# Expert layers of a two-block transformer: how many down units are kept during routing, and which engine builds the gated one-hot rows

## The chip, the cores and the metric

The kernel runs on one core of a Trainium2 chip. The metric is the device time of one execution in microseconds. Three executions of the kernel before gave 3460.87, 3461.62 and 3469.74 us; the median is 3461.62 us. Engines are named as the profile names them: PE (matmul) with PEld (its weight loads), DVE (vector), ACT (scalar), POOL (GpSimd), SP (which issues the DMAs).

## The reference, cut to what matters

Two layers of a first block, each a mixer and an expert layer, are followed by two layers of a second block (feed-forward, mixer, feed-forward). The change is in the expert layers alone. An expert layer scores 256 tokens against two sets of 128 sub-keys in 8 heads, takes the best 16 pairs in each head, and for those experts (16384 = 128 x 128 in all) computes a gated sum:

```python
def chunk(xi):
    q = (xi @ w_query).reshape(B, PEER_CHUNK, PEER_HEADS, 2, PEER_HALF)
    s = jnp.einsum('bthpd,hpnd->bthpn', q, sub_keys)
    s1, i1 = lax.top_k(s[..., 0, :], PEER_TOPK)
    s2, i2 = lax.top_k(s[..., 1, :], PEER_TOPK)
    cand = (s1[..., :, None] + s2[..., None, :]).reshape(...)
    top_s, top_c = lax.top_k(cand, PEER_TOPK)
    idx = (jnp.take_along_axis(i1, top_c // PEER_TOPK, axis=-1) * PEER_N_KEYS
           + jnp.take_along_axis(i2, top_c % PEER_TOPK, axis=-1))
    g = jax.nn.softmax(top_s.astype(jnp.float32), axis=-1)
    u = jnp.take(expert_down, idx, axis=0)
    act = jax.nn.gelu(jnp.einsum('btd,bthkd->bthk', xi, u).astype(jnp.float32))
    v_sel = jnp.take(expert_up, idx, axis=0)
    return jnp.einsum('bthk,bthkd->btd', (g * act).astype(xi.dtype), v_sel)
```

## The kernel before, in words

Nothing is gathered. The kernel computes the down projection of all 16384 experts for all 256 tokens, multiplies it by a gate that is zero for the experts that a token did not choose, and projects all of it up. Expert number 128*i1 + i2 belongs to unit i2; a unit is a block of 128 experts, one 512 KB load of weights (`raw`), split by ACT into a high part `whi` (L93) and by DVE into a low part `wlo` (L97), and 24 matmuls (three products, L170 to L172, for each of 8 chunks of the model width).

One expert layer (`peer`, L488) runs in these stages:

- **Routing.** 16 query units and their scores, then a long chain of small DVE instructions (maxima, indices, gates), which ends in the tile `it` (L610): for each token its 128 selected pairs as two key numbers and a gate. PE has little to do in that chain, so the first `N_STORE` = 64 units of the down projection are computed meanwhile (`down_pair`, two units to a PSUM bank). ACT takes each pair through the gelu into `ca` (L614), which stays in SBUF.
- **One-hot loop** (L622). The gates are expanded in 64 groups of four tokens. For each token a row block `oa` (selected pair against key number, 1 where the first key number is that column, L631, DVE) and a row block `ob` (the gate where the second key number is that column) are built, 128 x 128 each, by comparing `iota` with a column of `it`. `ob` takes one DVE instruction a token (L636, two per-partition operands) or two ACT instructions (L633, L634): by `by_act` (L628) ACT has the groups whose number leaves 1 when divided by `N_ACT` = 3, which is 21 of 64, DVE the other 43. PE multiplies the two (L639) into a PSUM bank `gps`: the gates of four tokens for all experts. DVE multiplies the part of the first `N_STORE` units into `ca` (L641), and ACT copies the rest into `gg` (L642). `oa` and `ob` have `OH` = 3 buffers each, `gps` rotates over four banks. L641 can't begin before all of `ca` is there.
- **Units after the loop.** For the units from `N_STORE` on, `down_pair` leads to the gelu in place (L665) and a DVE product into `gg` (L667). The first two pairs (`N_PARK`) use the banks that the up projection will accumulate in, and can run beside the loop. Then 32 (first expert layer) or 40 (second) steps of `Mod.step` are due (L670): each loads 512 KB of `w_mod` through the same three `raw` buffers and gives PE 4 matmuls (L940); they compute modulation vectors of the second block and are what PE has to fill the one-hot loop with. After that pairs of down units alternate with up units (`up`, L652), which lag `N_LAG` = 16 units behind.

The order of the instructions on each engine is fixed when the kernel is built, by a planner that goes by priorities and its own estimate of times; on the chip each engine goes through its list in order and waits by semaphores.

Of the kernel before, what the change touches and what calls it, by code (L numbers as in the profile page):

```python
# [19 lines left out]
NDC = 8  # L20
EPS = 1e-6
NEG = -1.0e30
N_STORE = 64
N_LAG = 16
N_PARK = 2
N_MOD = 32
# [2 lines left out]
PAT_1 = "gggv"  # L29
PAT_0 = "gv"  # L30
M_BUFS = 3
N_ACT = 3
OH = 3
AB = 3
AHEAD = 0
# [452 lines left out]
def peer(n: Net, layer, mod, mod_upto):  # L488
    nc, d = n.nc, n.d
    pre = f"l{layer}_"  # L490
    NS = N_STORE
    n.stream.pattern = PAT_R
    with ExitStack() as st:
# [6 lines left out]
        def down_pair(i, sink, tag=None):  # L500
            b = n.bank("dn", tag).rearrange("p (u t) -> p u t", u=2)
            for u in range(2):
                w = n.unit(d[pre + "down"][i + u])
                n.proj_t(b[:, u], w, xn, first=u == 0)
            sink(b)

        with ExitStack() as sr:
# [44 lines left out]
            for a0, a1, wb, o in CAND:  # L552
                na = a1 - a0
                nc.vector.tensor_tensor(
                    out=cand[:, :, o:o + na * wb].rearrange("p h (a b) -> p h a b", b=wb),
                    in0=v4[:, :, 0, a0:a1].unsqueeze(3).to_broadcast([128, 16, na, wb]),
# [56 lines left out]
            for i in range(0, NS, 2):  # L613
                down_pair(i, lambda b: nc.scalar.activation(  # L614
                    out=ca[:, i:i + 2], in_=b, func=AF.Gelu_apprx_tanh), "ac")

        with ExitStack() as sg:
            gp = sg.enter_context(n.tc.tile_pool(name="gg", bufs=1, reuse_waits="tile"))
            gg = gp.tile([128, 128 - NS, T], F32, name="gg")
            onehot = n.tc.tile_pool(name="oneh", bufs=OH, reuse_waits="tile")  # L620
            o2 = onehot.__enter__()
            for t0 in range(0, T, 4):  # L622
                a = o2.tile([128, 4, 128], F32, tag="oa", name="oa")
                b = o2.tile([128, 4, 128], F32, tag="ob", name="ob")
                g = n.bank("gps").rearrange("p (t e) -> p t e", t=4)


                by_act = t0 // 4 % N_ACT == 1  # L628
                for t in range(4):
                    at = lambda s: it[:, s, t0 + t:t0 + t + 1]  # L630
                    nc.vector.tensor_scalar(out=a[:, t], in0=n.iota, scalar1=at(0), scalar2=None, op0=OP.is_equal)  # L631
                    if by_act:
                        nc.scalar.activation(out=b[:, t], in_=n.iota, func=AF.Abs, scale=-1.0, bias=at(1))  # L633
                        nc.scalar.activation(out=b[:, t], in_=b[:, t], func=AF.Relu, scale=-2.0, bias=at(2))  # L634
                    else:
                        nc.vector.tensor_scalar(out=b[:, t], in0=n.iota, scalar1=at(1), scalar2=at(2),  # L636
                                                op0=OP.is_equal, op1=OP.mult)
                for t in range(4):
                    nc.tensor.matmul(g[:, t], a[:, t], b[:, t], start=t == 0, stop=True, skip_group_check=True)  # L639
                ge = g.rearrange("p t e -> p e t")  # L640
                nc.vector.tensor_tensor(out=ca[:, :, t0:t0 + 4], in0=ca[:, :, t0:t0 + 4], in1=ge[:, 0:NS], op=OP.mult)  # L641
                nc.scalar.copy(out=gg[:, :, t0:t0 + 4], in_=ge[:, NS:128])  # L642
            n.stream.pattern = PAT_G
            onehot.__exit__(None, None, None)
            g2 = sg.enter_context(n.tc.tile_pool(name="gg2", bufs=2, reuse_waits="tile"))

            def coef(i):
                return ca[:, i] if i < NS else gg[:, i - NS]

            acc = []  # L650

            def up(i):  # L652
                if not acc:
                    acc.extend(n.accs())
                w = n.unit(d[pre + "up"][i])
                c = coef(i)
                ch = g2.tile([128, T], F32R, tag="ch", name="ch")
                cl = g2.tile([128, T], F32R, tag="cl", name="cl")
                n.split(c, ch, cl)
                n.up(acc, w, (ch, cl), i == 0, i == 127)  # L660

            done = 0
            for i in range(NS, 128, 2):
                def sink(b):
                    nc.scalar.activation(out=b, in_=b, func=AF.Gelu_apprx_tanh)  # L665
                    c = gg[:, i - NS:i - NS + 2]
                    nc.vector.tensor_tensor(out=c, in0=c, in1=b, op=OP.mult)  # L667
                if i == NS + 2 * N_PARK:
                    while mod.next < mod_upto:
                        mod.step(n.main.raw_p)  # L670
                    mod.bank = None
                down_pair(i, sink, "ac" if i < NS + 2 * N_PARK else None)
                while i >= NS + 2 * N_PARK and done < i + 2 - N_LAG:
                    up(done)
                    done += 1
            while done < 128:
                up(done)
                done += 1
            n.residual(n.x, acc)
# [765 lines left out]
def two_blocks_kernel(ctx: ExitStack, tc: tile.TileContext, d, out, stages=None):  # L1445
# [12 lines left out]
    for s in stages:  # L1458
        with tc.tile_pool(name="xn", bufs=1, reuse_waits="tile") as n.xn_p:
            if s in ("mix0", "mix1"):  # L1460
                with n.psum(ac=4, mm=3, fl=1), tc.tile_pool(name="mod", bufs=M_BUFS, reuse_waits="tile") as p:
                    with n.low():
                        aside(mods[0], p, M_0 if s == "mix0" else M_1)
                    (hgrn_gmlp if s == "mix0" else mla_moba)(n)
            elif s.startswith("peer"):
                with n.psum(ac=4, mm=2, m2=2):
                    peer(n, int(s[4]), mods[1], N_MOD if s[4] == "0" else 72)
            elif s.startswith("mod"):
                with n.psum(ac=4, mm=2, fl=2), tc.tile_pool(name="mod", bufs=3, reuse_waits="tile") as p:
                    aside(mods[int(s[3])], p, 72)  # L1470
            elif s.startswith("ffn"):
                w, l = int(s[3]), int(s[5])
                with n.psum(ac=4, mm=2, m2=2):
                    ffn(n, n.x, mods[l], 0, 0 if w == 1 else 6, d[f"f{w}i{l}"], d[f"f{w}o{l}"],
                        n.v(f"norm_g{l}")[:, (w - 1) * 16:(w - 1) * 16 + 8], s)
            elif s == "mixb0":
                with n.psum(ac=4, mm=2, fl=2):
                    window_gla(n, mods[0])
            elif s == "mixb1":
                with n.psum(ac=4, mm=2, m2=2):  # L1480
                    pool_mix(n, mods[1])
            elif s == "final":
                with n.psum(ac=4, mm=2, m2=2):
                    final_norm(n, out)
# [154 lines left out]
```

## Time and profile before

| | us |
|---|---|
| median of three executions | 3461.62 |
| the profiled execution, its own time | 3467.64 |
| its span (first to last instruction) | 3465.9 |
| PE busy / DVE busy / ACT busy / POOL busy | 3313.4 / 2193.9 / 1649.2 / 179.0 |
| one-hot stretch of the first expert layer, after its stored units | 441 to 565 |
| one-hot stretch of the second expert layer, after its stored units | 1529 to 1661 |

The profile is one execution. Times within it are microseconds from the start of the span, unless they are marked ns. Busy time of PE counts the time from a matmul's start to its end, with many matmuls under way at once, so a busy PE need not be at its full rate; the spacing of starts shows the rate. The chain of waits puts 83% of the span on PE and 11% on DVE. Some records of small instructions are missing in a trace (of 64 `ca` products of the first one-hot stretch 61 are listed).

### The profile page before, as it was taken

How to read it: one execution, taken by the hardware profiler on the slowest of the kernel's cores; microseconds unless marked ns; L12 is line 12 of the kernel's file. 1: busy time of each engine (PE TensorE's matmuls, PEld its weight loads, DVE VectorE, ACT ScalarE, POOL GpSimd, SP SyncE). 2: the span in 40 equal slices, each digit the busy share in tenths (PEclk: the TensorE clock that was granted, in tenths of full speed). 3: DMA queues.
4: the chain of work that ended last, by engine and by line, in shares of the span. 5: the costliest groups of instructions: out<-in, count | busy, mean ns of one | idle time of the engine just before them, and what ended most of it. 6: DMA issues, size and time to landing. Idle time of an engine off the chain costs nothing.

```text
span 3465.9 us, 65621 instructions
## 1 busy us (share of the span) xinstructions
PE 3313.4 (96%) x26734; PEld 3150.2 (91%) x26734; DVE 2193.9 (63%) x4589; ACT 1649.2 (48%) x2609; POOL 179.0 (5%) x93
## 2 busy tenths in 40 slices
PE   7999998999999999998999999999999989999798
PEld 6789977999999779996899999999999779999698
DVE  6389487555556559759555555666766656666665
ACT  5445455444444344445445444544644444454443
POOL 2200000000000310000000000100000020100200
PEclk9999999999999999999999999999999999999899
DMA  6645544556555545545556555554444235454353
GB/s 227 230 159 182 178 156 161 183 183 207 183 183 170 199 157 166 177 158 182 195 183 231 183 183 183 182 183 143 158 165 147 86 123 187 165 183 156 132 187 105
DMA packets 165759, 597.79 MB, mean 172 GB/s; under 512 B 18512, under 2 KB 20176, under 8 KB 165072
## 3 DMA queue, kind: packets, MB, share of 16 engines
q1 hardware_dynamic: 165456, 593.59, 51.5%
q8 instruction: 210, 3.44, 0.4%
q14 instruction: 93, 0.76, 0.1%
HBM read 592.47 MB, written 1.05 MB: 171 GB/s over the span
## 4 chain that ended last, share of the span: by engine, by line
PE 83%; DVE 11%; DMA 2%; ACT 2%; issue 1%; POOL 0%; SPq 0%; ACTq 0%; DVEq 0%; POOLq 0%
PE acc L170 11%; PE acc L171 10%; PE acc L172 10%; PE dn L172 7%; PE dn L170 7%; PE dn L171 7%; PE ff L170 6%; PE ff L171 6%; PE ff L172 6%; DVE wlo L97 2%; PE mm L170 2%; PE mm L171 2%; PE mm L172 2%; PE mod L940 2%; DMA mraw<-w_mod 2%; PE gps L639 2%
## 5 line engine op out<-in xcount | busy, mean ns | idle before, releaser
L93 ACT CAST whi<-raw 128x1024 fp32r<-128x1024 f32 x973 | 1016.3, 1046 | 1398.9 <-PE acc L171 540.7
L97 DVE TENSOR_TENSOR wlo<-raw,whi 128x1024 fp32r<-128x1024 f32 x908 | 1111.6, 1225 | 841.8 <-ACT whi L93 841.3
L170 PE MATMUL dn<-xnh,whi 128*128 128x256 f32 x2048 | 582.3, 284 | 3.1 <-ACT gg L642 2.5
L172 PE MATMUL dn<-xnh,wlo 128*128 128x256 f32 x2048 | 581.8, 285 | 1.5 <-DVE wlo L97 1.5
L171 PE MATMUL dn<-xnl,whi 128*128 128x256 f32 x2048 | 581.5, 284 | 0.0
L171 PE MATMUL acc<-cl,whi 128*128 128x256 f32 x2048 | 561.6, 283 | 1.0 <-DVE cl L165 1.0
L172 PE MATMUL acc<-ch,wlo 128*128 128x256 f32 x2048 | 559.5, 283 | 0.0
L170 PE MATMUL acc<-ch,whi 128*128 128x256 f32 x2048 | 512.2, 283 | 0.2 <-DVE gg L667 0.2
L170 PE MATMUL ff<-xnh,whi 128*128 128x258 f32 x1760 | 504.6, 287 | 7.5 <-ACT rstd L216 4.0
L171 PE MATMUL ff<-xnl,whi 128*128 128x258 f32 x1760 | 502.8, 286 | 4.2 <-DVE xnl L247 4.2
L172 PE MATMUL ff<-xnh,wlo 128*128 128x258 f32 x1760 | 499.2, 284 | 3.5 <-POOL wlo L97 2.2
L170 PEld LDWEIGHTS dn<-xnh,whi 128*128 128x128 f32 x2048 | 395.0, 193 | 3.7 <-ACT gg L642 2.7
L172 PEld LDWEIGHTS dn<-xnh,wlo 128*128 128x128 f32 x2048 | 394.4, 193 | 2.2 <-DVE wlo L97 2.2
L171 PEld LDWEIGHTS dn<-xnl,whi 128*128 128x128 f32 x2048 | 395.0, 193 | 0.0
L171 PEld LDWEIGHTS acc<-cl,whi 128*128 128x128 f32 x2048 | 393.2, 192 | 1.5 <-DVE cl L165 1.5
L172 PEld LDWEIGHTS acc<-ch,wlo 128*128 128x128 f32 x2048 | 392.1, 192 | 0.0
L170 PEld LDWEIGHTS acc<-ch,whi 128*128 128x128 f32 x2048 | 363.7, 192 | 0.4 <-DVE gg L667 0.4
L170 PEld LDWEIGHTS ff<-xnh,whi 128*128 128x128 f32 x1760 | 334.8, 190 | 12.2 <-ACT rstd L216 5.2
L171 PEld LDWEIGHTS ff<-xnl,whi 128*128 128x128 f32 x1760 | 337.0, 192 | 6.3 <-DVE xnl L247 5.6
L172 PEld LDWEIGHTS ff<-xnh,wlo 128*128 128x128 f32 x1760 | 335.1, 191 | 4.9 <-POOL wlo L97 2.7
L97 POOL TENSOR_TENSOR wlo<-raw,whi 128x1024 fp32r<-128x1024 f32 (+1 forms) x65 | 157.7, 2433 | 2614.0 <-ACT whi L93 1968.6
L171 PE MATMUL acc<-hl,whi 128*128 128x256 f32 x880 | 246.9, 282 | 3.0 <-DVE hl L1017 3.0
(446 smaller groups left out, 5389.5 us busy)
## 6 DMA issues: line engine op xcount, KB each, us to landing
raw<-l_down SPq DMA_DIRECT2D x256, 512.0 KB, 3.4
raw<-l_up SPq DMA_DIRECT2D x256, 512.0 KB, 3.3
mraw<-w_mod SPq DMA_DIRECT2D x144, 512.0 KB, 4.4
raw<-f1i SPq DMA_DIRECT2D x132, 512.0 KB, 3.4
raw<-f2i SPq DMA_DIRECT2D x88, 512.0 KB, 3.9
raw<-f1o SPq DMA_DIRECT2D x66, 512.0 KB, 3.3
raw<-w_t SPq DMA_DIRECT2D x46, 512.0 KB, 3.6
raw<-f2o SPq DMA_DIRECT2D x44, 512.0 KB, 4.1
```

The source lines that it names most:

```text
L93: nc.scalar.copy(hi[:, 0:k], raw[:, 0:k])
L97: eng.tensor_tensor(out=low[:, 0:k], in0=raw[:, 0:k], in1=hi.bitcast(F32)[:, 0:k], op=OP.subtract)
L170: mm(out, w[0], x[0], start=first, stop=False, skip_group_check=True)
L171: mm(out, w[0], x[1], start=False, stop=False, skip_group_check=True)
L172: mm(out, w[1], x[0], start=False, stop=last, skip_group_check=True)
L639: nc.tensor.matmul(g[:, t], a[:, t], b[:, t], start=t == 0, stop=True, skip_group_check=True)
L940: nc.tensor.matmul(ps[32 * j:32 * j + 32], n.cond[:, k], raw[:, j * T:(j + 1) * T], start=k == 0, stop=k == NDC - 1, tile_position=(0, 32 ...
```

## The change

Three edits. `N_STORE` goes from 64 to 40: 24 units of each expert layer move from the stage before the one-hot loop to the stage after it, `ca` becomes 40 units wide and `gg` 88. `N_ACT` goes from 3 to 4: ACT builds `ob` for 16 groups of 64 instead of 21. The other 48 groups' `ob` (before: 43 groups) are built by POOL instead of DVE, with the same instruction, one for each token.

```diff
-N_STORE = 64
+N_STORE = 40
...
-N_ACT = 3
+N_ACT = 4
...
                     else:
-                        nc.vector.tensor_scalar(out=b[:, t], in0=n.iota, scalar1=at(1), scalar2=at(2),
+                        nc.gpsimd.tensor_scalar(out=b[:, t], in0=n.iota, scalar1=at(1), scalar2=at(2),
                                                 op0=OP.is_equal, op1=OP.mult)
```

## Rows read from the trace of the kernel before

**Rows 1.** Busy time by stretch: each engine's us (instructions), PEclk, DMA share, GB/s.
```profile
275.00:300.00 25.00, 25.00 (x211) 25.00 (x210) 24.49 (x113) 13.52 (x16) 0.00 (x0) 1.00 0.66 210
400.00:440.00 40.00, 40.00 (x336) 40.00 (x335) 16.83 (x15) 18.16 (x21) 0.00 (x0) 1.00 0.54 181
480.00:500.00 20.00, 16.47 (x116) 10.07 (x115) 16.27 (x71) 10.04 (x33) 0.00 (x0) 0.83 0.48 161
540.00:560.00 20.00, 16.56 (x129) 12.53 (x130) 20.00 (x87) 15.53 (x46) 0.00 (x0) 1.00 0.46 154
700.00:800.00 100.00, 100.00 (x835) 100.00 (x835) 54.56 (x66) 45.73 (x65) 0.00 (x0) 1.00 0.61 205
1620.00:1640.00 20.00, 17.35 (x155) 12.49 (x154) 20.00 (x88) 11.81 (x39) 0.00 (x0) 1.00 0.65 211
1640.00:1660.00 20.00, 14.84 (x111) 8.49 (x110) 12.70 (x50) 5.90 (x18) 0.00 (x0) 0.82 0.48 162
```
**Rows 2.** Groups of instructions, 441 to 565: count, busy us, mean ns, idle before.
```profile
L631 DVE TENSOR_SCALAR oa<-iota,it 128x128 f32<-128x128 f32 x233 | 59.7, 276 | 1.1 <-PE gps L639 1.1
L636 DVE TENSOR_SCALAR ob<-iota,it 128x128 f32<-128x128 f32 x157 | 52.8, 336 | 0.0
L641 DVE TENSOR_TENSOR ca<-ca,gps 128x256 f32<-128x256 f32 x61 | 24.8, 410 | 9.6 <-PE gps L639 9.6
L97 DVE TENSOR_TENSOR wlo<-raw,whi 128x1024 fp32r<-128x1024 f32 x4 | 4.8, 1213 | 0.0
...
L639 PE MATMUL gps<-ob,oa 128*128 128x128 f32 x484 | 76.8, 295 | 5.7 <-DVE ob L636 3.6 <-ACT gg L642 1.4 <-ACT ob L633 0.6
L940 PE MATMUL mod<-mraw,cond 128*32 128x256 f32 x256 | 24.8, 404 | 7.4 <-DMA mraw<-w_mod 7.4
```
**Rows 3.** Order of time on DVE inside a group: start, us.
```profile
523.50 0.28 DVE L631 TENSOR_SCALAR oa<-iota,it 128x128 f32<-128x128 f32 x1
523.70 0.34 DVE L636 TENSOR_SCALAR ob<-iota,it 128x128 f32<-128x128 f32 x1
523.96 0.28 DVE L631 TENSOR_SCALAR oa<-iota,it 128x128 f32<-128x128 f32 x1
...
525.06 0.41 DVE L641 TENSOR_TENSOR ca<-ca,gps 128x256 f32<-128x256 f32 x1
525.39 0.34 DVE L636 TENSOR_SCALAR ob<-iota,it 128x128 f32<-128x128 f32 x1
```
**Rows 4.** The last of routing, and the first and last stored units' evictions.
```profile
L610 DVE COPY it<-tp x4: 547/552/558, 341.4 to 1427.2; 128x384 f32<-128x384 f32 x4
...
357.87 1.05 ACT L93 CAST whi<-raw 128x1024 fp32r<-128x1024 f32 x1 [1.09 <-PE dn L171]
360.75 1.05 ACT L93 CAST whi<-raw 128x1024 fp32r<-128x1024 f32 x1 [1.83 <-PE dn L171]
...
L614 ACT ACTIVATE ca<-dn x64: 585/594/602, 261.7 to 1530.3; 128x512 f32<-128x512 f32 x64
```
**Rows 5.** POOL by line: min/median/max ns; then single splits in order of time.
```profile
L1172 POOL TENSOR_TENSOR sg<-sg,sb x4: 741/901/1191, 2508.8 to 2512.7; 128x256 f32<-128x256 f32 x4
...
1106.33 2.40 POOL L97 TENSOR_TENSOR wlo<-raw,whi 128x1024 fp32r<-128x1024 f32 x1 [948.34 <-ACT whi L93]
...
1134.26 2.37 POOL L97 TENSOR_TENSOR wlo<-raw,whi 128x1024 fp32r<-128x1024 f32 x1 [3.73 <-ACT whi L93]
...
1147.16 1.84 POOL L97 TENSOR_TENSOR wlo<-raw,whi 128x768 fp32r<-128x768 f32 x1 [5.04 <-ACT whi L93]
```
**Rows 6.** DVE and POOL in the same microseconds, in order of time.
```profile
1108.93 0.48 DVE L739 TENSOR_SCALAR kq<-ang 128x256 f32<-128x256 f32 x2
1109.34 2.69 DVE L741 TENSOR_SCALAR kq<-kq 128x256 f32<-128x256 f32 x2
1111.94 0.48 DVE L742 TENSOR_SCALAR kq<-kq 128x256 f32<-128x256 f32 x2
...
1109.15 2.52 POOL L97 TENSOR_TENSOR wlo<-raw,whi 128x1024 fp32r<-128x1024 f32 x1 [0.42 <-ACT whi L93]
```
**Rows 7.** ACT's rows of the one-hot loop, then DVE's product after it.
```profile
525.30 1.26 ACT L634 ACTIVATE ob<-ob,it 128x128 f32<-128x128 f32 x4
...
L642 ACT COPY gg<-gps x128: 346/368/398, 446.6 to 1657.8; 128x256 f32<-128x256 f32 x128
...
L667 DVE TENSOR_TENSOR gg<-gg,dn 128x512 f32<-128x512 f32 x64 | 43.3, 680 | 0.4 <-ACT gg L642 0.4
```
**Rows 8.** PE: 24 one-hot products in a row, and three down matmuls after the loop.
```profile
449.36 2.84 PE L639 MATMUL gps<-ob,oa 128*128 128x128 f32 x24
...
565.11 0.58 PE L170 MATMUL dn<-xnh,whi 128*128 128x256 f32 x1 [2.52 <-ACT gg L642]
565.49 0.41 PE L171 MATMUL dn<-xnl,whi 128*128 128x256 f32 x1
565.71 0.41 PE L172 MATMUL dn<-xnh,wlo 128*128 128x256 f32 x1
```
**Rows 9.** Second expert layer: the last `ob` row, PE's waits for `w_mod` (1529 to 1661).
```profile
1649.77 0.33 DVE L636 TENSOR_SCALAR ob<-iota,it 128x128 f32<-128x128 f32 x1
...
PE mod L940 <- DMA mraw<-w_mod: 10.1, 12, 1.7
...
mraw<-w_mod SPq DMA_DIRECT2D x40, 512.0 KB, 4.4
```

## The prediction

> **What bounds the kernel now.** I read the page first (PE busy nearly everywhere, POOL 5%), then the busy time by stretch through one expert layer, because a change in one stage is worth what that stage waits for. Three kinds of stretch show [rows 1]. From 275 to 440, with the stored down units, and from 700 to 800, with down and up units, PE is busy all the time at a granted clock of 1.00 (its 2.4 GHz level): PE is the bound, and what DVE or ACT do there is covered; DVE is at 24.49 of 25 us during routing, 16.83 of 40 after it, 54.56 of 100 in the late stage. In the one-hot stretch PE's share falls (16.56 of 20) and DVE stands at 20.00 of 20: here DVE is the bound. These stretches are 441 to 565 and 1529 to 1661, 124 and 132 us, and only they can become shorter or longer by much.
>
> DVE's account of the first one, by the spacing of starts [rows 3], since durations overlap: an `oa` row takes 0.20 us (523.50 to 523.70), an `ob` row 0.26 (523.70 to 523.96), a `ca` product 0.33 (525.06 to 525.39). Five of 64 groups are multiplied before 441 (20 `oa` rows), so 236 `oa`, 160 `ob` (157 listed) and 64 `ca` remain [rows 2]: 47 + 41 + 21 = 109 us, with four splits of 1.2 and some 3 us of small work 117 us. Of 124 us, 7 are left for waits. In the second layer the same 117 us lie in 132: the last `ob` row starts at 1649.77, and what follows waits for `w_mod` [rows 9]. So there DVE is the bound up to about 1650, loads after it.
>
> **The change part by part.**
>
> *24 units move behind the loop.* A unit costs PE 2.88 us (split to split, 357.87 to 360.75) [rows 4]. The stored units end 24 x 2.88 = 69 us earlier, near 372 instead of 441. Routing ends at about 342, second layer 1428 (`it`, [rows 4]) against 1529. The cover had 98 and 101 us to spare, so about 29 and 32 us remain: no routing is laid bare, cost 0. Were the cover gone, each missing unit would cost 2.88 us. The 24 units come back after the loop at the same 2.88, in the stage where PE is full already: 0 net. There they cost DVE 12 products more (L667, 680 ns [rows 7]), 8.2 us a layer beside a DVE that is half idle: 0. The gelu is the same size in either place. On SP's queue their 24 loads move behind the 32 or 40 `w_mod` loads; queue and buffers are the same, 0. The loop itself only moves earlier.
>
> *Narrower `ca`, wider `gg`.* L641 goes from 256 to 160 columns; from 256 to 512 columns DVE's product rises from 410 to 680 ns [rows 2, 7], 1.05 ns a column, so 0.10 us is saved 64 times: 6 us of DVE a layer. L642 goes from 256 to 352 columns: by ACT's 368 ns for 256 [rows 7] and 594 for 512 [rows 4] 0.085 us more, 5 us of ACT a layer.
>
> *ACT's share.* ACT has 16 groups instead of 21. An ACT group is 8 rows at 0.30 us (1.26 us for four with overlap [rows 7]), 2.4 us, so 12 us less. ACT was not the bound; worth 0 alone.
>
> *`ob` goes to POOL.* DVE loses all 160 rows of the stretch, 41 us. POOL, idle through the whole expert layer (948 us before its next instruction [rows 5]), gets 48 groups x 4 = 192 rows a layer; of the five early groups four are POOL's, so 176 remain. No row shows this instruction on POOL, so I bound it. POOL's nearest forms have two inputs: 256 columns in 0.741 at the shortest, 768 in 1.84, 1024 in 2.37 us [rows 5], that is 2.15 ns a column and 0.19 us fixed. At 128 columns it makes 0.47 with two inputs, and 0.33 if one input costs half as much a column. The two per-partition operands cost something too: on DVE a second one makes 336 ns out of 276 [rows 2], 0.06 each, which gives 0.33 + 0.12 = 0.45. Upper end: the 128x256 row, 0.74. I take 0.45, where the two roads meet, and keep 0.33 to 0.74.
>
> *POOL and DVE do not run side by side.* [Rows 6] show the price. Two DVE instructions of the kind of `oa` (SBUF to SBUF, `tensor_scalar`) take 0.48 us together just before and just after, but 2.69 while POOL's split of 1109.15 runs, and they finish 0.36 us after it. POOL's split in turn takes 2.52 instead of 2.37, held by the DVE pair in front of it. So each `oa` row holds POOL up: at most its whole spacing, 0.20, at least nothing; a 256-column one held it 0.15, I take 0.13 for 128.
>
> The Trainium skill says the same in "SBUF — State Buffer", section "Summary: rules for kernel authors": a VectorE instruction in a two-port mode and a GpSimd instruction exclude each other for a whole instruction, and the second one "fully blocks"; "Perfetto Trace Analysis", section "Optimizing Scalar/DVE Operations", concludes that moving work between these two might not help. The rows agree with the first by the 2.69 us; the second is the slower rival's direction.
>
> The new account of the stretch is therefore a sum over both engines: 176 x 0.45 = 79, 236 x 0.13 = 31, four weight splits of 1.2 us (two SBUF inputs) 5: 115 us, against DVE's 117 before. DVE's own list is far shorter now (47 + 64 x 0.23 + 8 = 70 us if nothing blocked it), and ACT's about 65. Gain 2 to 3 us a layer, about 5 in all: nearly nothing.
>
> *The wait that is added.* PE's one-hot products now wait for POOL's rows. Queued behind them on PE are the `w_mod` matmuls and the parked down pairs, both of which only fill the stretch; behind a blocked `oa` row on DVE is the `ca` product, for which ACT's copy and the PSUM bank wait. Three row buffers and four banks take up a few microseconds of that, which is in the 7 us of waits that I leave as they are.
>
> Sum against the profiled execution's own time: 3467.64 - 5 = 3462.6. That execution lies 6.0 us above the median of the runs shown (3461.62), so on the median's level the forecast is **3457 us**. About 0.3%, 10.4 us, is what a measurement of this kernel can tell from no change.
>
> **The rivals.** All are one variable, the POOL row. Two layers x 176 rows make 352 us of time per us of row, as long as the pair of engines is the bound.
>
> *Slower: the POOL row is the new bound.* If it costs 0.60, the stretch takes 106 + 31 + 5 = 142 us, 25 more in the first layer and as much in the second, about +48 in all: 3505. At 0.74 it is 166 us, +97: 3554. PE would idle more, and with idling its granted clock falls (0.83 at 480 to 500, at times the 1.2 GHz level [rows 1]); matmuls then start 0.22 us apart, as at 565.49, instead of the 0.12 that 24 a unit of 2.88 make [rows 4, 8]. It decides from 0.46 upward, and shows from 0.49. For it: POOL's splits are twice DVE's (2.37 against 1.21 [rows 2, 5]), and two operations with two operands have no row here. Against: half the inputs of the nearest row.
>
> *Faster: the row is cheap.* At 0.33 the pair of engines needs 58 + 31 + 5 = 94 us. The next bounds are close to that: PE has about 484 products at 0.12 (24 in 2.84 [rows 8]), 57 us, 25 us of `w_mod` matmuls and 12 of parked units, 94 us [rows 2]; in the second layer 40 loads of 0.52 MB at the 211 GB/s of its best stretch [rows 1, 9] need 100 us and the parked units 10 more. That is 24 and 21 us less than the accounts now, 45 in all: 3417.
> The Trainium skill leans this way: "GPSIMD Engine Reference", section "Engine selection", calls one-input work roughly line-rate on GpSimd; an estimate by that page's 1.2 GHz is 0.11 us of streaming above the fixed 0.19, which would put the row at 0.30 before its operands. No run here shows it.
>
> *It doesn't show at all:* the loop's order on PE is laid by the planner, and `w_mod` loads that arrive in bursts set the pace whoever builds the rows; then the time is that of before, 3462.
>
> **How the numbers follow.** A row of 0.40 to 0.50: 35%, 3439 to 3475 by 352 us per us around 3457; that is the forecast with its own range. Above 0.50: 34%. Below 0.40: 24%. Nothing to be seen: 7%. The forecast's 35% split into 12 faster, 20 same, 3 slower; with the rivals' and the last case's 3% near the bound: faster 0.38, same 0.25, slower 0.37. The range goes down to 3417 (4% below) and up to a row of 0.67, 3457 + 352 x 0.22 = 3534 (15% above).
>
> **What would show it.** In the changed profile: POOL's `ob` rows at 0.4 to 0.5 us when undisturbed and `oa` rows on DVE stretched far above 276 ns with POOL running; DVE's busy time in the stretch still near full although it lost 41 us of work; the stretch beginning near 372 and lasting 115 to 125 us, with PE waiting on POOL `ob`; PE full before and after it; routing still ended before the stored units. Wrong would be: `oa` rows that stay at 276 ns beside POOL (no exclusion), a POOL row outside 0.33 to 0.74, or PE idle before the loop (the cover gone).

## The result, and the profile after

The changed kernel takes 3539.67 us (median of 4 executions, 3538.09 to 3541.55) where the kernel before takes 3461.47: a ratio of 1.022, 95% interval 1.0203 to 1.0238. It is 78 us slower, 83 us above the 3457 us of the prediction and 6 us above the upper end of its range. The profiled execution has a span of 3537.0 us, 71.1 more than before.

Where the 71 us lie can be read from two marks that both traces have: the end of routing (the first and last copy into `it`, L610) and POOL's first weight split of the second mixer, which is the first sign that the first expert layer is over. Kernel after, one line of the code and one of POOL's list (start, us):

```profile
L610 DVE COPY it<-tp x4: 547/552/557, 343.9 to 1466.5; 128x384 f32<-128x384 f32 x4
...
1144.44 2.40 POOL L97 TENSOR_TENSOR wlo<-raw,whi 128x1024 fp32r<-128x1024 f32 x1 [608.71 <-ACT whi L93]
```

Before, these marks stood at 341.4, 1106.33 and 1427.2 [rows 4, 5]. From routing to the mixer it was 764.9 us and is 800.5 (1144.44 - 343.9): +35.6. The mixer and the second routing were 320.9 and are 322.1: unchanged. 2.5 us were lost ahead of the first mark, so what remains of the 71.1, some 32 us, is the second expert layer and what follows it.

A third mark times the one-hot loop itself: ACT copies one part of each of the 64 groups into `gg` (L642), and a line of these copies ends with the first and the last start. Kernel before, first and second expert layer, then kernel after:

```profile
L642 ACT COPY gg<-gps x64: 347/367/398, 446.6 to 572.6; 128x256 f32<-128x256 f32 x64
L642 ACT COPY gg<-gps x64: 346/369/398, 1534.5 to 1657.8; 128x256 f32<-128x256 f32 x64
...
L642 ACT COPY gg<-gps x64: 427/452/460, 377.4 to 540.1; 128x352 f32<-128x352 f32 x64
L642 ACT COPY gg<-gps x64: 427/452/460, 1499.5 to 1666.1; 128x352 f32<-128x352 f32 x64
```

From first to last copy the loop took 126.0 and 123.3 us and takes 162.7 and 166.6: 37 and 43 us more. Both expert layers pay, and about equally.

The busy time by stretch (us and instructions of PE, PEld, DVE, ACT, POOL; PEclk, DMA share, GB/s), kernel after:

```profile
300.00:340.00 40.00, 40.00 (x336) 40.00 (x336) 37.24 (x42) 18.11 (x22) 0.00 (x0) 1.00 0.55 174
360.00:380.00 20.00, 20.00 (x171) 20.00 (x171) 10.35 (x22) 11.15 (x20) 6.39 (x7) 1.00 0.51 170
420.00:440.00 20.00, 15.56 (x144) 9.32 (x142) 9.55 (x43) 7.85 (x23) 16.11 (x21) 1.00 0.85 283
460.00:480.00 20.00, 17.94 (x70) 14.57 (x70) 9.49 (x41) 8.29 (x24) 20.00 (x25) 0.59 0.07 25
480.00:500.00 20.00, 16.62 (x68) 13.45 (x68) 10.26 (x43) 8.60 (x25) 20.00 (x26) 0.67 0.00 1
600.00:700.00 100.00, 100.00 (x836) 100.00 (x835) 54.17 (x64) 45.75 (x65) 0.00 (x0) 1.00 0.59 199
...
376.00:541.00 165.00, 133.85 (x892) 101.74 (x891) 81.87 (x323) 71.06 (x194) 150.85 (x183) 0.86 0.36 122
```

Compared with [rows 1]: PE is full up to 380, so the stored units still cover routing, and full again from 600. Between them the one-hot stretch begins near 376, 65 us earlier than before, and lasts to 541: 165 us instead of 124. DVE, which was at 20.00 of 20 there, is at 9 to 10; POOL, which did nothing, is at 20.00 of 20 from 460 on. PE has 70 instructions in 20 us instead of 129. All 70 are one-hot products; of the 129 from 540 to 560 in the kernel before, 95 were, and the rest were `w_mod` matmuls. The loads of `w_mod` are over by 460, so nothing is left to fill the stretch with, and PE's granted clock, which was 1.00 up to 440, has a mean of 0.59 from 460 to 480, between its two levels (1.2 and 2.4 GHz).

The same stretch by groups (count | busy us, mean ns | idle before) and its longest waits (us in total, times, longest), to be held against [rows 2]; then POOL's rows in both layers (min/median/max ns) and the last part of its list in the first (start, us). Kernel after:

```profile
L636 POOL TENSOR_SCALAR ob<-iota,it 128x128 f32<-128x128 f32 x183 | 152.3, 844 | 8.9 <-PE gps L639 8.8
L631 DVE TENSOR_SCALAR oa<-iota,it 128x128 f32<-128x128 f32 x238 | 59.1, 326 | 0.0
L641 DVE TENSOR_TENSOR ca<-ca,gps 128x160 f32<-128x160 f32 x64 | 20.2, 316 | 74.4 <-PE gps L639 74.3
L639 PE MATMUL gps<-ob,oa 128*128 128x128 f32 x488 | 101.8, 348 | 15.1 <-POOL ob L636 12.0 <-ACT ob L634 2.4
...
DVE ca L641 <- PE gps L639: 74.3, 34, 3.8
ACT gg L642 <- DVE ca L641: 58.5, 44, 3.4
PEld gps L639 <- POOL ob L636: 30.1, 65, 2.1
...
POOL ob L636 <- PE gps L639: 8.8, 4, 2.7
...
L636 POOL TENSOR_SCALAR ob<-iota,it x384: 782/788/2457, 344.6 to 1661.0; 128x128 f32<-128x128 f32 x192
...
449.15 86.57 POOL L636 TENSOR_SCALAR ob<-iota,it 128x128 f32<-128x128 f32 x104 [2.22 <-PE gps L639]
```

POOL's 183 rows take 152 of the 165 us and POOL waits for only 9; from 449 on 104 rows follow each other without a pause. Everybody else waits along one chain: DVE's `ca` products for PE (74 us, where it was 9.6), PE for POOL's rows. An `ob` row costs 0.844 us in this stretch in the mean, and the median of all is 0.788; I had priced it at 0.45.

### The profile page after: what moved, and what is told of

It is laid out like the page before. It is cut to its first block, busy times and chain, and to the rows that moved or that the text cites. A ratio compares the mean times of both kernels' runs of the same rounds, so it can differ in the third digit from the quotient of the medians.

```text
span 3537.0 us, 65700 instructions
## 1 busy us (share of the span) xinstructions
PE 3351.3 (95%) x26734; PEld 3179.5 (90%) x26734; DVE 2126.9 (60%) x4269; ACT 1638.2 (46%) x2529; POOL 502.4 (14%) x477
## 3 DMA queue, kind: packets, MB, share of 16 engines
HBM read 592.47 MB, written 1.05 MB: 168 GB/s over the span
## 4 chain that ended last, share of the span: by engine, by line
PE 48%; DVE 2%; ACT 1%; issue 1%; DMA 0%; SPq 0%; ACTq 0%; DVEq 0%
PE acc L171 7%; PE acc L172 7%; PE acc L170 6%; PE ff L170 6%; PE ff L171 6%; PE ff L172 6%; PE dn L172 2%; PE dn L170 2%; PE dn L171 2%; PE mm L170 1%; PE mm L171 1%; PE mm L172 1%; PE nps L226 1%; PE sc L1296 0%; DVE wlo L97 0%
## 5 line engine op out<-in xcount | busy, mean ns | idle before, releaser
L171 PE MATMUL acc<-cl,whi 128*128 128x256 f32 x2048 | 570.9, 284 | 1.9 <-DVE cl L165 1.9
L172 PE MATMUL acc<-ch,wlo 128*128 128x256 f32 x2048 | 569.7, 284 | 0.0
L170 PE MATMUL acc<-ch,whi 128*128 128x256 f32 x2048 | 538.3, 284 | 4.3 <-ACT ch L164 3.5
L636 POOL TENSOR_SCALAR ob<-iota,it 128x128 f32<-128x128 f32 x384 | 324.1, 856 | 413.4 <-DVE it L610 351.3
L170 PEld LDWEIGHTS acc<-ch,whi 128*128 128x128 f32 x2048 | 375.4, 193 | 5.5 <-ACT ch L164 3.9
```

Of the source, the lines that this page charges most:

```text
L170: mm(out, w[0], x[0], start=first, stop=False, skip_group_check=True)
L171: mm(out, w[0], x[1], start=False, stop=False, skip_group_check=True)
L172: mm(out, w[1], x[0], start=False, stop=last, skip_group_check=True)
L636: nc.gpsimd.tensor_scalar(out=b[:, t], in0=n.iota, scalar1=at(1), scalar2=at(2), op0=OP.is_equal, op1=OP.mult)
```

## The experiments

The theory after the result (A): the POOL row is dear by itself and paces the loop. Its rivals: the moved units cost something (B); the row is cheap but DVE's rows hold it up (C); the order of PE's products and the `w_mod` loads pace the loop and POOL only looks busy (D).

**The parts one by one.** 40 stored units alone:

```diff
-N_STORE = 64
+N_STORE = 40
```

> The kernel before with one edit: 40 stored units instead of 64; DVE and ACT build the rows as before. Theory A (the cost lies in the POOL rows): the moved units are covered on both sides, the time stays within 10 us of before, the one-hot stretch begins near 372 and lasts 118 to 124 us in the first expert layer (DVE has 6 us less of ca products). Rival B (the moved units cost): the loop now meets a colder or worse filled PE and the time rises by 20 us or more.

Measured: 3448.1 us against 3464.26 of the kernel before on the same chip, ratio 0.996 (0.9944 to 0.9977). B falls, the other way round even: this edit is a gain of 16 us (8 to 19 by its interval), more than the 10 that theory A had allowed. The stretch by 20 us and the `ca` group of its loop (380 to 480), kernel with 40 units:

```profile
420.00:440.00 20.00, 18.01 (x157) 13.06 (x158) 20.00 (x93) 13.87 (x43) 0.00 (x0) 1.00 0.58 198
...
L641 DVE TENSOR_TENSOR ca<-ca,gps 128x160 f32<-128x160 f32 x53 | 17.5, 331 | 7.7 <-PE gps L639 7.7
```

DVE is still the bound there, and its products take 331 ns instead of 410 [rows 2]: 64 x 0.08 = 5 us a layer. The gain lies in the one-hot loops: from the first to the last copy into `gg` they take 116.4 and 110.1 us here, where they took 126.0 and 123.3, together 23 us less. What shortened them beyond the 5 us of products was not traced further.

POOL's rows alone, with 64 stored units (the changed kernel with the first line of the change undone):

```diff
-N_STORE = 40
+N_STORE = 64
```

> The changed kernel with 64 stored units, so only the rows move to POOL and ACT has 16 groups. Theory A: the time is that of the changed kernel, 3525 to 3550 us, with 176 POOL rows of about 0.8 us after the stored units, 140 us or more of POOL work in a stretch of 155 to 170 us. Rival B: if the moved units carry the loss, it falls back towards 3462 to 3480 us.

Measured: 3546.56 us, ratio 1.0232 (1.0215 to 1.0249). The whole loss is in the rows. Whether the 40 units take a little of it back can't be told from the times (the changed kernel's interval, 1.0203 to 1.0238, overlaps); by the copies into `gg` the loops are longer here, 171.7 and 173.0 us against 162.7 and 166.6. With 171.7 us the first one is also just above the 155 to 170 expected.

ACT's share alone (DVE builds the other 48 groups):

```diff
-N_ACT = 3
+N_ACT = 4
```

> The kernel before with ACT taking 16 groups instead of 21 and DVE the other 48; 64 stored units. DVE gets 20 rows more a layer at 0.26 us, 5 us in a loop whose bound is DVE's list: 3468 to 3476 us. If ACT's rows were what the loop waited for, it would fall below 3455 us.

Measured: 3472.17 us against 3461.62, ratio 1.0029 (1.0016 to 1.0042): 10.6 us, as expected for 20 rows more a layer on the engine that is the bound.

**The price of the row by itself.** A kernel that times POOL's forms in stretches of their own (one execution):

```diff
+        for w in (128, 256, 512, 1024):
+            for i in range(12):
+                g.tensor_scalar(out=dst[i % 4][:, 0:w], in0=src[0][:, 0:w], scalar1=at(0), scalar2=at(1),
+                                op0=OP.is_equal, op1=OP.mult)
+            end()
...
+            g.tensor_scalar(..., scalar1=at(0), scalar2=None, op0=OP.is_equal)
...
+            g.tensor_scalar(..., scalar1=2.0, scalar2=1.0, op0=OP.is_equal, op1=OP.mult)
...
+            g.tensor_tensor(..., op=OP.subtract)
```

> Only the final normalization is kept of the computation; ahead of it POOL runs stretches of 12 rows alone: tensor_scalar with two per-partition operands at 128, 256, 512 and 1024 columns, then at 128 columns with one operand, with constants, and a two-input product; then 24 rows beside 96 DVE rows of the oa form, and 24 beside 16 DVE subtractions of two 128x1024 SBUF tiles. Theory A (the row is dear by itself): 0.75 to 0.80 us at 128 columns alone, less than 10% more beside DVE's rows. Rival C (the row costs about 0.45 us and DVE's rows hold it up to 0.8): 0.40 to 0.55 alone, 0.7 to 0.9 beside them. If the per-partition operands carry it, the row with constants falls under 0.5 us; if the columns carry it, 256 columns cost over 1.2 us.

The groups of POOL by shape (L1464 two operations and two operands, L1468 one of each, L1472 two constants, L1476 two inputs; busy us, mean ns), then the two engines side by side (min/median/max ns), same kernel:

```profile
L1464 POOL TENSOR_SCALAR dst<-src,sv 128x1024 f32<-128x1024 f32 x12 | 45.2, 3780 | 0.6 <-DVE sv L1457 0.6
L1464 POOL TENSOR_SCALAR dst<-src,sv 128x512 f32<-128x512 f32 x12 | 24.7, 2073 | 0.6 <-DVE sv L1457 0.6
L1464 POOL TENSOR_SCALAR dst<-src,sv 128x256 f32<-128x256 f32 x12 | 14.4, 1220 | 0.6 <-DVE sv L1457 0.6
L1464 POOL TENSOR_SCALAR dst<-src,sv 128x128 f32<-128x128 f32 x12 | 9.3, 794 | 12.1 <-DVE sv L1457 12.1
L1472 POOL TENSOR_SCALAR dst<-src 128x128 f32<-128x128 f32 x12 | 7.3, 642 | 0.0
L1468 POOL TENSOR_SCALAR dst<-src,sv 128x128 f32<-128x128 f32 x12 | 7.0, 604 | 0.6 <-DVE sv L1457 0.6
L1476 POOL TENSOR_TENSOR dst<-src,src 128x128 f32<-128x128 f32 x12 | 5.0, 455 | 0.1
...
L1479 POOL TENSOR_SCALAR dst<-src,sv x24: 788/966/3512, 128.4 to 153.7; 128x128 f32<-128x128 f32 x24
L1482 DVE TENSOR_SCALAR dvd<-src,sv x96: 272/276/390, 128.2 to 148.3; 128x128 f32<-128x128 f32 x96
L1486 POOL TENSOR_SCALAR dst<-src,sv x24: 787/788/8440, 158.4 to 185.1; 128x128 f32<-128x128 f32 x24
```

The row costs 0.794 us with nothing beside it. On the price of the row alone A holds and C falls. From 512 to 1024 columns the time rises by 1.71 us, 3.3 ns a column, with 0.37 us fixed; by the sign named beforehand (1.22 us at 256 columns, over 1.2) the columns carry it, and they are 0.43 of the 0.79 at 128. So it isn't half of the two-input form, it is dearer: the two-input product of 128 columns takes 0.455, the compare alone 0.604, the compare and product with constants 0.642. With constants the row does not fall under 0.5 us, so the per-partition operands are not the main part: the two together carry 0.15 of the 0.79. If each carries half of that, the second operation costs about 0.11; that split is an estimate. A's other expectation failed: beside 96 DVE rows without a pause the median rises to 966 ns, 22% and not under 10%, about 0.04 us for each of the four or five DVE rows that go by. DVE's rows hardly notice: 96 of them start 0.21 us apart. The longest POOL rows of these two stretches (3.5 and 8.4 us) ran beside DVE's two-input subtractions.

**Who excludes whom.** A second one of this sort (one execution), because [rows 6] had shown a DVE `tensor_scalar` blocked by POOL:

```diff
+            g.tensor_tensor(out=dst[i % 4], in0=src[0], in1=src[1], op=OP.subtract)
...
+            g.tensor_scalar(out=dst[i % 4], in0=src[0], scalar1=at(0), scalar2=at(1),
+                            op0=OP.is_equal, op1=OP.mult)
...
+            nc.vector.tensor_tensor(out=dvd[i % 4], in0=src[0], in1=src[1], op=OP.add)
```

> Only the final normalization is kept of the computation; ahead of it three stretches of POOL beside DVE: 12 two-input 128x1024 products beside 60 DVE rows of the oa form; 8 tensor_scalar rows of 1024 columns beside 96 such DVE rows; 12 tensor_scalar rows of 128 columns beside 6 DVE subtractions with two SBUF inputs. Theory E (what excludes DVE's rows is POOL's two-input form): DVE's rows wait up to 2.4 us in the first stretch and stay at 0.27 to 0.30 us in the second, and in the third POOL waits for DVE. Rival F (any POOL instruction excludes them, short ones just do it briefly): DVE's rows wait up to 3.8 us in the second stretch too.

The lines of the three stretches (min/median/max ns), then DVE's instructions while POOL ran the first and the second:

```profile
L1465 POOL TENSOR_TENSOR dst<-src,src x12: 2333/2335/2431, 12.8 to 38.1; 128x1024 f32<-128x1024 f32 x12
L1467 DVE TENSOR_SCALAR dvd<-src,sv x60: 274/275/2377, 12.7 to 49.5; 128x128 f32<-128x128 f32 x60
L1471 POOL TENSOR_SCALAR dst<-src,sv x8: 3902/4121/4121, 50.6 to 79.2; 128x1024 f32<-128x1024 f32 x8
L1474 DVE TENSOR_SCALAR dvd<-src,sv x96: 271/274/1124, 50.5 to 80.9; 128x128 f32<-128x128 f32 x96
L1478 POOL TENSOR_SCALAR dst<-src,sv x12: 787/788/3926, 84.0 to 98.4; 128x128 f32<-128x128 f32 x12
L1481 DVE TENSOR_TENSOR dvd<-src,src x6: 1211/1218/1309, 84.0 to 89.7; 128x1024 f32<-128x1024 f32 x6
...
12.80:40.40 27.60, 27.60 (x13) 1.00 0.00 0
50.60:81.10 30.50, 30.50 (x96) 1.00 0.00 0
```

Beside POOL's two-input products 13 DVE rows fit into 27.6 us, one to a product, and wait up to 2.38 us. Beside POOL's one-input rows of even greater length all 96 fit into 30.5 us; most take 274 ns, a few up to 1.12 us, and POOL's row grows from 3.78 to 4.12. F falls: no DVE row waits anything like 3.8 us. E holds for most rows only, since it said that all would stay at 0.27 to 0.30 us: around each change from one POOL row to the next, DVE's starts are twice about a microsecond apart (0.91 and 1.05 us, otherwise 0.20), so that the 96 rows need 0.32 us each instead of 0.20. Why DVE pauses there is open. In the third stretch POOL's row waits for DVE's two-input subtractions (up to 3.9 us; 8.4 in the kernel above) and DVE's don't wait.

**Cheaper and fewer rows in the loop.** The changed kernel with the gate left out of POOL's rows:

```diff
-                        nc.gpsimd.tensor_scalar(out=b[:, t], in0=n.iota, scalar1=at(1), scalar2=at(2),
-                                                op0=OP.is_equal, op1=OP.mult)
+                        nc.gpsimd.tensor_scalar(out=b[:, t], in0=n.iota, scalar1=at(1), scalar2=None,
+                                                op0=OP.is_equal)
```

> The changed kernel whose POOL rows compare only and leave the gate out (one operation, one operand; 3 of 4 groups then have ungated experts, so this part of the result is left out). Alone such a row took 0.58 us instead of 0.78. Theory A (the POOL row paces the loop): 180 rows a layer x 0.2 us = 36 us less a layer while POOL is the bound, 3475 to 3490 us. Rival D (the order of PE's products and w_mod loads paces the loop, POOL only looks busy): within 15 us of the changed kernel, 3525 us or more.

Measured: 3448.95 us, ratio to before 0.9971 (0.9958 to 0.9985). That is 86 us less than the changed kernel by the two ratios (0.9971 and 1.022), and below the 3475 to 3490 expected. POOL's rows in the one-hot stretch (376 on), this kernel:

```profile
L636 POOL TENSOR_SCALAR ob<-iota,it 128x128 f32<-128x128 f32 x177 | 111.8, 650 | 4.9 <-PE gps L639 4.9
```

650 ns instead of 844: 0.19 us a row, 34 us for 177 rows. 43 us a layer were saved, more than the 36 expected: some 9 us beyond the rows themselves, of which POOL's shorter waits (4.9 instead of 8.9) are a part and the rest is open. The loops agree: from first to last copy into `gg` 121.6 and 123.6 us, 41 and 43 less than in the changed kernel. D falls clearly.

ACT with half of the groups, so that POOL has 128 rows a layer instead of 192:

```diff
-N_ACT = 4
+N_ACT = 2
```

> The changed kernel (40 stored units) with ACT taking 32 of 64 groups instead of 16, so POOL has 128 rows a layer instead of 192. Theory A (POOL's rows pace the loop at about 0.85 us): 64 rows less save up to 54 us a layer until the next list binds; that is ACT with 32 x 2.4 + 64 x 0.45 = 105 us or POOL with its remaining 109, so the loop comes to 110 to 120 us and the time to 3440 to 3465 us. Rival D (the loop's length is set by PE's order and the w_mod loads): above 3510 us.

Measured: 3456.99 us, ratio to before 0.9993 (0.9981 to 1.0005), inside the range given. Two stretches of its first loop:

```profile
400.00:420.00 20.00, 18.36 (x159) 12.04 (x156) 11.66 (x53) 14.56 (x47) 16.88 (x21) 1.00 0.76 246
480.00:500.00 20.00, 16.37 (x118) 14.33 (x118) 10.06 (x43) 16.08 (x50) 14.53 (x18) 1.00 0.00 1
```

64 rows less save about 40 us a layer, less than their 54. The loop itself is longer than the 110 to 120 us expected: 126.6 and 126.0 us from first to last copy into `gg`. And no list is full in these two stretches, neither ACT's (16.08 of 20) nor POOL's (14.53), so what bounds this version is waits between the engines, and which of them was not settled.

**Versions between.** POOL may still be worth a small share. Of every 8 groups 3 to DVE, 3 to ACT, 2 to POOL, with 64 stored units:

```diff
-N_ACT = 3
+PAT_B = "vagvavag"
...
-                by_act = t0 // 4 % N_ACT == 1
+                by = PAT_B[t0 // 4 % len(PAT_B)]
...
-                    if by_act:
+                    if by == "a":
...
-                        nc.vector.tensor_scalar(out=b[:, t], in0=n.iota, scalar1=at(1), scalar2=at(2),
+                        eng = nc.gpsimd if by == "g" else nc.vector
+                        eng.tensor_scalar(out=b[:, t], in0=n.iota, scalar1=at(1), scalar2=at(2),
...
```

> The kernel before (64 stored units), of every 8 groups 2 have their gated rows on POOL, 3 on ACT, 3 on DVE (43 DVE groups become 24, 21 ACT groups 24, POOL 16). If POOL rows cost 0.8 us and hardly disturb DVE: POOL needs 16 x 4 x 0.8 = 51 us, ACT 24 x 2.4 + 25 = 83, DVE 47 + 21 + 25 + 8 = 101 instead of 117, so about 15 us less a layer in the first and less in the second (loads of w_mod): 3430 to 3450 us. If a POOL row holds DVE's rows for its whole length, DVE's list grows by 51 us and the time rises to 3480 us or more.

Measured: 3448.9 us, ratio 0.9959 (0.9945 to 0.9973). At the upper edge of what was expected without exclusion. ACT's share rose with it, from 21 groups to 24, so this gain is that of the whole split; POOL's part in it was not measured by itself.

The same with 40 stored units, and a third with 3 groups of 8 on POOL (`PAT_B = "gavgavga"`):

```diff
-N_STORE = 64
+N_STORE = 40
```

> 40 stored units together with the split of 3 DVE, 3 ACT and 2 POOL groups of 8. If both gains come from DVE's list in the one-hot loop (6 us of ca products, about 20 of gated rows a layer) they add until PE's own 94 us bind: 3425 to 3440 us. If the second bound is already reached by either one: 3445 to 3450 us, as each alone.

> 40 stored units with 3 POOL, 3 ACT and 2 DVE groups of 8. POOL's 96 rows of 0.85 us make 82 us, DVE's list 47 + 15 + 17 + 8 = 87, ACT's 86, PE's 94: all below the loop before, so 3425 to 3440 us, no slower than with 2 of 8. If POOL's rows hold DVE's or come late for PE, it lies above the 2 of 8 version by 10 us or more.

Measured: 3429.21 us with 2 of 8, ratio 0.9911 (0.9892 to 0.993); 3439.82 with 3 of 8, ratio 0.9935 (0.9912 to 0.9958). The two gains add (0.996 x 0.9959 = 0.992). The third group on POOL brings no gain and may cost: its median lies 10.6 us above, which was the sign named for POOL's rows holding DVE's or coming late for PE, but the two intervals overlap. A stretch of the loop with 2 of 8:

```profile
420.00:440.00 20.00, 18.29 (x171) 13.94 (x168) 19.12 (x87) 14.71 (x48) 10.79 (x12) 1.00 0.65 223
```

PE gets 171 instructions through in 20 us, 101 of them one-hot products, where the kernel before had 95 such products from 540 to 560 and the changed kernel 70 from 460 to 480. DVE is at 19.12 of 20, so its list is again close to the bound. This version beats both kernels: 0.9% faster than before, 3.0% faster than the changed one by the two ratios (0.9911 / 1.022).

## Why the prediction was wrong, point by point

- *What bounds the kernel* was read rightly: the one-hot stretch alone became longer, PE is full on both sides of it, and in [rows 1] DVE was its bound (moving 20 rows to DVE cost 10 us, taking 5 us of products away helped).
- *24 units move behind the loop, cost 0.* Routing stayed covered: `it` begins at 343.9, the loop near 376 (predicted 372). By itself the edit even gains 16 us, of which the next term explains 10.
- *Narrower `ca`, wider `gg`.* 6 us of DVE a layer were predicted, 0.08 us x 64 = 5 measured; a `gg` copy rose by 0.084 us where 0.085 was worked out. The sum had no place for the gain, since it took POOL and DVE's exclusion for the bound; with POOL as the bound, that was right.
- *ACT's share, worth 0 alone.* Right for ACT's own list. But its five groups go to the engine that is the bound: on DVE they cost 10 us in two layers; on POOL they are 20 of its rows, which the prediction had counted in its 192.
- *The POOL row at 0.45 us* is the step that failed: the term 176 x 0.45 = 79 us. The row is 0.79 alone, 0.844 in the loop, above even the upper end of 0.74. The two-input price was read well (0.47 worked out from [rows 5], 0.455 measured), but the step from it to the row, that one input costs half as much a column, had no row behind it and was wrong in sign: 3.3 ns a column against 2.15. That "the two roads meet" near 0.45 confirmed nothing, since both start from the two-input form. The second operation had been given no price on POOL: the 0.06 us between DVE's 276 and 336 ns [rows 2] are a second operand and a second operation together, and the prediction read them as the operand alone. 176 rows x 0.34 us = 60 us a layer.
- *Exclusion, 236 x 0.13 = 31 us.* Too large. [Rows 6] are a two-input POOL instruction, and that form does shut DVE's rows out; the form of this change does not. In the loop DVE's `oa` rows take 326 instead of 276 ns in the mean, and POOL's row 0.844 instead of 0.794: 183 x 0.05 = 9 us. Most rows are not held at all (median 0.788); three that ran beside DVE's weight splits took 1.5 to 2.5 us and make a third of the 9. DVE's busy time, which should have stayed near full, fell to half (9.49 of 20 from 460 to 480). So the 9 stand against the 31 of exclusion and the 5 of weight splits together: 27 us less than predicted.
- *The added wait* was named rightly (PE on POOL's rows, 30 us on its weight loads), and put at no cost beyond the old 7 us; POOL in turn waits 9 us for PE, all of it before 450, while the `w_mod` matmuls still stand in PE's list.
- Together, for the first layer: 115 and the 7 of waits predicted, + 60 for the price of the row, + 6 for seven more rows than the 176 (183 x 0.79), - 27, + 2 for POOL's 9 us of waits instead of 7: 163, of 165 us measured. That the miss stayed 6 us beyond the range is luck in part: the price of the row alone would have made 3457 + 352 x 0.34 = 3577, and the other errors, the exclusion priced too high above all, took 37 of it away.
- *The rivals.* The slower one was the case, with its mechanism, its place and its sign (PE idling, the granted clock falling to 0.59). Its sum is too high, 3554 for a row of 0.74 where a row of 0.79 measured 3540, because it carried the 31 us of exclusion; the range ended at a row of 0.67, and so just short. In the faster rival the bound by loads was too tight: it took 211 GB/s as the best, and the changed kernel reaches 283 from 420 to 440.

The Trainium skill's "GPSIMD Engine Reference", section "Engine selection", calls one-input work on GpSimd roughly line-rate. That does not fit here: the row streams at 3.3 ns a column, and at 128 columns it takes 0.794 us on POOL against 0.336 on DVE [rows 2]. The Trainium skill's rule in the same section, to give elementwise work to VectorE and not to GpSimd, fits these two numbers. The Trainium skill's "SBUF — State Buffer", section "Who interferes with whom", says that a VectorE instruction in a two-port mode and a GpSimd instruction shut each other out for a whole instruction. With POOL's two-input products the runs agree (DVE's rows wait up to 2.38 us); with its one-input rows the same DVE rows are not shut out (96 rows in 30.5 us). The Trainium skill's clause there, that a VectorE instruction with two SBUF inputs contends with a GpSimd instruction that reads SBUF, agrees: one POOL row took 8.4 us beside them.

## What to carry to other kernels

An instruction that moves to another engine has to be priced on that engine in its own form: the number of operations, of inputs and of operands each change the price, and a neighbouring form, even a "heavier" one, bounds it on neither side. When the bound of a stretch is a list of small instructions, give the slow engine only so many of them that its list stays shorter than the others': here, with 64 stored units, a split with 8 rows of 32 on POOL gains 0.4%, and one with 24 of 32 loses 2.3%. A range whose one open price has no row should reach past the dearest neighbouring form.

## What the runs showed of the hardware that was not expected

- POOL's compare-and-multiply of 128x128 with two per-partition operands takes 0.794 us, longer than its two-input product (0.455), and by size 1.22, 2.07 and 3.78 us at 256, 512 and 1024 columns.
- A POOL `tensor_scalar`, which has one input, lets DVE's `tensor_scalar` rows of 128 columns through: 0.21 us apart beside rows of 128 columns, 0.32 beside rows of 1024, against 0.20 undisturbed. A POOL product with two inputs of 1024 columns lets through one of them a product.
- DVE instructions with two SBUF inputs, one behind the other, can keep a POOL row waiting for 8.4 us; in the loop the longest `ob` row took 2.46 us.
